# The first two output-projection groups summed in HBM, by accumulating DMAs

## The chip, the cores and the metric

The kernel runs on one core of a Trainium2 chip. The metric is device time in microseconds (us) of one execution, lower is better.

## What is computed

One layer of a decoder trunk on x of 1024 tokens by 1024 channels, all in float32. Cut to what matters here:

```python
h = rms_norm(x, norm_mix_g); z = h @ w_in
y_pool = pooling_mixer(z[:, :512])                 # 4 groups of 128 channels
y_attn = rms_norm(diff_attention(q, k, v)) * 0.8   # 4 heads of 128 channels
y = concat(y_pool, y_attn)                         # 1024 x 1024
x = x + y @ w_out                                  # the output projection
h = rms_norm(x, norm_ffn_g)
gu = h @ ffn_w_in; g = conv3(gu[:, :2816]); u = gu[:, 2816:]
x = x + (silu(g) * u) @ ffn_w_out
return rms_norm(x, norm_final_g)
```

## The kernel before

Every matrix product is done as three float32r products of a high and a low part ("split": a ScalarE cast gives the high part, a subtraction on GpSimd or VectorE the low part). The work goes through five stages.

1. **Start.** Eight row tiles of x (128 tokens each, 512 KB) are loaded by SP (line 169, four buffers), normalised (lines 114 to 130) and transposed by TensorE into hTh and hTl (lines 132 to 140). The order of the first loads is written out in LOADS (line 35): x0, g, x1, x2, the weights q0 and k0, small parameters, x3, v0. Rows x4 to x7 follow when a buffer is free. The first three projections (first_units, lines 237 to 257) run on row tiles as they arrive, in two halves of 512 tokens.
2. **Projections, attention and pooling**, in the order of PLAN (line 37).
3. **Output projection** (out_rows, line 530). The eight 128-channel pieces of y are summed in three groups, OUT_GROUPS = ((3, 2), (1, 0, 4), (5, 6, 7)) (line 33), because the last head is ready last; groups 0 and 1 fill TensorE beside the attention of head 3. For each row tile t of a group, line 533 loads the running sum (x for group 0, the scratch tensor x1_d after that), TensorE computes two halves of 512 columns into PSUM, VectorE adds each half to the loaded tile (line 541), and for groups 0 and 1 ScalarE's queue stores the tile to x1_d (line 543). The row tiles rotate through four buffers (tag "x", line 523). The weights and y pieces of a group are split in out_weights (line 465).
4. **Second norm and the blocks for the up projection.** Group 2 runs row tile by row tile with norm2 (line 561): square sums, a store of the tile to x1_d (line 568), and the scaling in place (line 577). Then transposes give the blocks b11, b21, b22 and, from differences of two row tiles (pair_blocks, line 587), t1 to t4. The feed-forward up projection uses a seven-product scheme over these blocks (ffn_up, line 656); the weights of each of the 22 column tiles are loaded by SP as ru and rg (line 621, two buffers of tag "rw"), combined and split in up_weights (line 616). up_weights runs one column tile ahead of ffn_up (lines 689 to 694).
5. **Down projection** (ffn_down, line 740) and the final norm (finish, line 713).

The order of the instructions on each engine is not written by hand: a list scheduler simulates the program and puts the ready instruction of highest priority next, priority being program order apart from stretches marked high. A ready instruction that stands later in the program can so be issued before an earlier one that still waits; afterwards each engine's order is fixed. SP, ScalarE and GpSimd each issue their DMAs in their own order; a waiting instruction holds up what is behind it on its queue.

Of the kernel before, what the change touches and what calls it, by code (L numbers as in the profile page):

```python
# [9 lines left out]
F32 = mybir.dt.float32  # L10
F32R = mybir.dt.float32r
AF = mybir.ActivationFunctionType
ALU = mybir.AluOpType
PSUM = bass.MemoryType.PSUM

P = 128
S = 1024
D = 1024
KC = D // P
NT = S // P  # L20
# [9 lines left out]
DOWN = [3] * 6 + [4]  # L30
PRODUCTS = "1675243"
QK = 10
OUT_GROUPS = ((3, 2), (1, 0, 4), (5, 6, 7))
FIRST = ("q0", "k0", "v0")
LOADS = "x0 g x1 x2 q0 k0 s x3 v0"
# [7 lines left out]
def trunk_kernel(ctx, tc, x, norm_mix_g, w_in, pool_w, rows, line, rel_bias, w_out, norm_ffn_g,  # L43
                 ffn_w_in, ffn_w_out, norm_final_g, onehot, out):
    nc = tc.nc
    x, out, w_in, w_out = x[0], out[0], w_in[0], w_out[0]
# [4 lines left out]
    x1_d = nc.dram_tensor("x1_rows", (S, D), F32).ap()  # L51

    const = ctx.enter_context(tc.tile_pool(name="const", bufs=1))
# [8 lines left out]
    def slot(dt, name):  # L62
        return slots.tile([P, S], dt, tag="y", name=name)
# [78 lines left out]
    def mm3(ps, wh, wl, hh, hl, first, last):  # L142
        nc.tensor.matmul(ps, wh, hh, start=first, stop=False)  # L143
        nc.tensor.matmul(ps, wh, hl, start=False, stop=False)  # L144
        nc.tensor.matmul(ps, wl, hh, start=False, stop=last)  # L145


    nc.scalar.preload_act_table_set("natural_log_exp_and_others")
    ident = const.tile([P, P], F32, name="ident")
    make_identity(nc, ident)  # L150
    flip = const.tile([P, P], F32, name="flip")
# [35 lines left out]

    prm = const.tile([P, 96], F32, name="prm")
    gsub = const.tile([P, 1], F32, name="gsub")
    nlam = const.tile([P, 1], F32, name="nlam")  # L190

    def small_params():
# [20 lines left out]

    g_bc = att.tile([P, D], F32, tag="qk", bufs=QK, name="g_mix")
    hTh = [big.tile([P, 4, S], F32R, tag="h", name=f"hTh{q}") for q in range(2)]
# [16 lines left out]
    def first_bank(n, half):  # L232
        ps = (sc_ps if n == "v0" else mm_ps)(f"z_{n}_{half}")
        first_ps[n, half] = ps
        return ps

    def first_units(qt):
        half = qt // 2
        if half:
            if qt == 3:  # L240
                for n in FIRST:
                    proj_half(first_bank(n, 1), *first_w[n], 1)
                    with tc.high_priority():
                        first_evac[n](1, first_ps[n, 1])
            return
        for n in FIRST:
            if qt % 2 == 0:
                first_bank(n, half)
            ps = first_ps[n, half][:, (qt % 2) * 256:(qt % 2) * 256 + 256]
            wh, wl = first_w[n]  # L250
            cs = slice(qt * 256, qt * 256 + 256)
            for k in range(KC):
                mm3(ps, wh[:, k, :], wl[:, k, :], hTh[k // 4][:, k % 4, cs], hTl[k // 4][:, k % 4, cs],
                    k == 0, k == KC - 1)
            if qt % 2:
                with tc.high_priority():
                    first_evac[n](half, first_ps[n, half])
# [4 lines left out]
    def proj_half(ps, wh, wl, half):  # L262
        cs = slice(half * 512, half * 512 + 512)
        for k in range(KC):
            mm3(ps, wh[:, k, :], wl[:, k, :], hTh[k // 4][:, k % 4, cs], hTl[k // 4][:, k % 4, cs],
                k == 0, k == KC - 1)
# [9 lines left out]
    def q_sink(h):  # L276
        q = [att.tile([P, S], F32R, tag="qk", bufs=QK, name=f"q{h}_{c}") for c in range(2)]

        def evac(half, ps):
            cs = slice(half * 512, half * 512 + 512)  # L280
            for c in range(2):
                hi = q[c][64 * c:64 * c + 64, cs]
                lo = q[c][64 - 64 * c:128 - 64 * c, cs]
                src = ps[64 * c:64 * c + 64, :]
                nc.scalar.mul(hi, src, SC)
                nc.vector.scalar_tensor_tensor(lo, src, SC, hi.bitcast(F32), op0=ALU.mult, op1=ALU.subtract)
        return q, evac

    def k_sink(h):
        kh = [(slot(F32R, f"kh{h}_{c}") if h == 1 else  # L290
               att.tile([P, S], F32R, tag="qk", bufs=QK, name=f"kh{h}_{c}")) for c in range(2)]
        kl = slot(F32R, f"kl{h}") if h == 1 else att.tile([P, S], F32R, tag="qk", bufs=QK, name=f"kl{h}")

# [10 lines left out]
    def v_sink(h):  # L304
        vh = att.tile([P, S], F32R, tag="qk", bufs=QK, name=f"vh{h}")
        if h == 1:
            vl = slot(F32R, f"vl{h}")
        else:
            vl = att.tile([P, S], F32R, tag="pl" if h == 3 else "qk", bufs=3 if h == 3 else QK, name=f"vl{h}")
        vh, vl = [a.rearrange("p (t e) -> p t e", e=P) for a in (vh, vl)]  # L310
# [10 lines left out]
    for t in range(NT):  # L321
        if t == 1:
            first_w.update({n: split_w(first_raw[n], n) for n in FIRST})
            q0, first_evac["q0"] = q_sink(0)
            k0, first_evac["k0"] = k_sink(0)
            v0, first_evac["v0"] = v_sink(0)
            small_params()
        if t not in xs:
            xs[t] = load_x(t)
        xt = xs[t]  # L330
        sq = att.tile([P, S], F32, tag="pl", bufs=3, name=f"sq_{t}")
        r = row_rstd(xt, sq, f"m{t}")
        scale_rows(xt, xt, r, g_bc, t in SHARE)
        with tc.high_priority():
            to_channels(xt, hTh, hTl, t, "m")
        if t % 2 == 1:
            first_units(t // 2)

    yT = [None] * 8

# [124 lines left out]
    def out_weights(gi):  # L465
        wo = []
        for n, k in enumerate(OUT_GROUPS[gi]):
            raw = ws.tile([P, D], F32, tag="raw", bufs=1, name=f"wo_{k}") if gi == 0 else e_tile(F32, f"wo_{k}")
# [56 lines left out]
    def e_tile(dt, name):  # L525
        return wide.tile([P, S], dt, tag="e", bufs=2, name=name)

    x1 = [None] * NT

    def out_rows(gi, wo, t):  # L530
        ts = slice(t * P, (t + 1) * P)
        xt = x1[t] = x_tile(F32, f"x1_{gi}_{t}")
        nc.sync.dma_start(xt, (x1_d if gi else x)[ts, :])
        for half in range(2):
            cs = slice(half * 512, half * 512 + 512)
            ps = mm_ps(f"o_{gi}_{t}_{half}")
            for n, (yh, yl, wh, wl) in enumerate(wo):
                nc.tensor.matmul(ps, yh[:, ts], wh[:, cs], start=n == 0, stop=False)  # L538
                nc.tensor.matmul(ps, yh[:, ts], wl[:, cs], start=False, stop=False)  # L539
                nc.tensor.matmul(ps, yl[:, ts], wh[:, cs], start=False, stop=n == len(wo) - 1)  # L540
            nc.vector.tensor_tensor(xt[:, cs], xt[:, cs], ps, op=ALU.add)  # L541
        if gi < 2:
            nc.scalar.dma_start(x1_d[ts, :], xt)

    for s in OUT_PLAN.split():
        if s[0] == "w":
# [69 lines left out]
    def up_weights(ct):  # L616
        raw = []
        for n, c in (("u", NCT + ct), ("g", ct)):
            r = mid.tile([P, KC * P], F32, tag="rw", bufs=2, name=f"r{n}{ct}")
            src = ffn_w_in[:, c * P:(c + 1) * P].rearrange("(k p) c -> p k c", p=P)  # L620
            nc.sync.dma_start(r.rearrange("p (k c) -> p k c", c=P), src)
            raw.append(r)
        u, g = raw
        a11, a12, a21, a22 = u[:, 0:512], u[:, 512:1024], g[:, 0:512], g[:, 512:1024]
        sa = mid.tile([P, S], F32, tag="st", bufs=2, name=f"sa{ct}")
        sb = mid.tile([P, S], F32, tag="st", bufs=2, name=f"sb{ct}")
        s1, s2, s3, s4 = sa[:, 0:512], sa[:, 512:1024], sb[:, 0:512], sb[:, 512:1024]
        nc.gpsimd.tensor_tensor(s1, a21, a22, op=ALU.add)  # L628
        nc.vector.tensor_tensor(s2, s1, a11, op=ALU.subtract)  # L629
        nc.vector.tensor_tensor(s4, a12, s2, op=ALU.subtract)  # L630
        nc.gpsimd.tensor_tensor(s3, a11, a21, op=ALU.subtract)
        uh, ul = u_tile(F32R, f"uh{ct}"), u_tile(F32R, f"ul{ct}")
        split(uh, ul, u)
        gt = x_tile(F32R, f"gt{ct}")
        split(gt[:, 0:512], gt[:, 512:1024], a22, nc.vector)
        sh = []
        for n, t in (("a", sa), ("b", sb)):
            h, l = (u_tile if n == "a" else x_tile)(F32R, f"s{n}h{ct}"), u_tile(F32R, f"s{n}l{ct}")
            split(h, l, t, nc.vector)
            sh.append((blocks(h), blocks(l)))  # L640
        (ah, al), (bh_, bl_), (uh, ul), gb = sh[0], sh[1], (blocks(uh), blocks(ul)), blocks(gt)
        return {"1": (uh[:, 0], ul[:, 0], "b11"), "2": (uh[:, 1], ul[:, 1], "b21"), "3": (bh_[:, 1], bl_[:, 1], "b22"),
                "4": (gb[:, 0], gb[:, 1], "t4"), "5": (ah[:, 0], al[:, 0], "t1"), "6": (ah[:, 1], al[:, 1], "t2"),
                "7": (bh_[:, 0], bl_[:, 0], "t3")}
# [112 lines left out]
    ct = 0  # L757
# [68 lines left out]
```

## Time and profile before

| what | value |
|---|---|
| time, median of 3 runs | 1114.7 us (1113.57 to 1114.74) |
| the profiled execution, device time | 1115.49 us |
| its span in the profile | 1113.7 us |
| TensorE busy (PE) | 96% of the span |
| VectorE busy (DVE) | 66% |
| ScalarE busy (ACT) | 43% |
| GpSimd busy (POOL) | 31% |
| HBM read, written | 82.57 MB, 28.32 MB |

Outside the profiled span lie 1115.49 - 1113.7 = 1.8 us of the profiled execution. Its device time is 0.8 us above the median of the three runs. Busy shares are means over five stages with different limits, so the profile is read stage by stage.

### The profile page before, as it was taken

How to read it: one execution, taken by the hardware profiler on the slowest of the kernel's cores; microseconds unless marked ns; L12 is line 12 of the kernel's file. 1: busy time of each engine (PE TensorE's matmuls, PEld its weight loads, DVE VectorE, ACT ScalarE, POOL GpSimd, SP SyncE). 2: the span in 40 equal slices, each digit the busy share in tenths (PEclk: the TensorE clock that was granted, in tenths of full speed). 3: DMA queues.
4: the chain of work that ended last, by engine and by line, in shares of the span. 5: the costliest groups of instructions: out<-in, count | busy, mean ns of one | idle time of the engine just before them, and what ended most of it. 6: DMA issues, size and time to landing. Idle time of an engine off the chain costs nothing.

```text
span 1113.7 us, 13597 instructions
## 1 busy us (share of the span) xinstructions
PE 1066.6 (96%) x5011; PEld 884.0 (79%) x5011; DVE 732.3 (66%) x1213; ACT 475.9 (43%) x775; POOL 341.7 (31%) x240
## 2 busy tenths in 40 slices
PE   5999999999899997999999999999999999999997
PEld 4988888887677675878888888888888788888885
DVE  7556787877797689577657656755665655544545
ACT  5557476655752355244333443443344222111133
POOL 3232242433730247133312232221314322221211
PEclk9999999999899998999999999999999999999999
DMA  8010110110386742123122212222247632212112
GB/s 242 28 50 27 43 46 19 43 39 26 133 278 216 242 171 76 57 95 95 57 94 95 93 59 96 90 81 76 82 127 267 223 114 99 89 60 95 39 50 102
DMA packets 85990, 111.76 MB, mean 100 GB/s; under 512 B 3618, under 2 KB 66303, under 8 KB 85924
## 3 DMA queue, kind: packets, MB, share of 16 engines
q1 hardware_dynamic: 79300, 86.78, 24.4%
q10 hardware_dynamic: 6624, 24.12, 5.5%
q8 instruction: 39, 0.64, 0.2%
q14 instruction: 27, 0.22, 0.1%
HBM read 82.57 MB, written 28.32 MB: 100 GB/s over the span
## 4 chain that ended last, share of the span: by engine, by line
PE 81%; DVE 8%; issue 4%; DMA 3%; ACT 1%; POOL 1%; SPq 1%; DVEq 0%; ACTq 0%; POOLq 0%
PE p L650 36%; PE fo L747 7%; PE fo L749 7%; PE fo L748 7%; PE tpa L402 1%; PE z_q L144 1%; PE z_q L145 1%; PE z_q L143 1%; PE o L538 1%; PE o L539 1%; PE o L540 1%; PE z_p L143 1%; PE z_p L144 1%; PE z_p L145 1%; PE z_v L143 1%
## 5 line engine op out<-in xcount | busy, mean ns | idle before, releaser
L747 PE MATMUL fo<-w,a 128*128 128x512 f32 x352 | 137.3, 390 | 2.8 <-DVE xr L750 2.8
L750 DVE TENSOR_TENSOR xr<-xr,fo 128x512 f32<-128x512 f32 x112 | 75.9, 684 | 97.0 <-PE fo L749 96.3
L748 PE MATMUL fo<-w,a 128*128 128x512 f32 x352 | 137.0, 389 | 0.0
L749 PE MATMUL fo<-w,a 128*128 128x512 f32 x352 | 137.0, 389 | 0.0
L80 POOL TENSOR_TENSOR w<-rw,w 128x1024 fp32r<-128x1024 f32 x22 | 61.3, 2796 | 156.4 <-ACT w L79 151.1
L628 POOL TENSOR_TENSOR sa<-rg 128x512 f32<-128x512 f32 x22 | 32.9, 1495 | 209.8 <-DMA rg<-in_ffn_w_in_dram 201.3
L80 POOL TENSOR_TENSOR ul<-ru,uh 128x1024 fp32r<-128x1024 f32 x22 | 58.1, 2642 | 71.8 <-PE p L650 37.6
L747 PEld LDWEIGHTS fo<-w,a 128*128 128x128 f32 x352 | 66.1, 188 | 17.6 <-DVE xr L750 4.0
L749 PEld LDWEIGHTS fo<-w,a 128*128 128x128 f32 x352 | 66.1, 188 | 13.9
L748 PEld LDWEIGHTS fo<-w,a 128*128 128x128 f32 x352 | 66.1, 188 | 13.6
L79 ACT CAST a<-ra 128x1024 fp32r<-128x1024 f32 x22 | 23.1, 1051 | 118.8 <-DVE xr L750 64.1
L362 ACT ACTIVATE p<-p,nm 128x128 f32<-128x128 f32 (+7 forms) x64 | 49.6, 776 | 40.9 <-DVE nm L361 40.5
L650 PE MATMUL p<-t4h,gt 128*128 128x512 f32 x176 | 58.9, 396 | 1.7 <-DVE g L675 1.7
L629 DVE TENSOR_TENSOR sa<-sa,ru 128x512 f32<-128x512 f32 x22 | 39.9, 1814 | 21.1 <-POOL sa L628 21.1
L538 PE MATMUL o<-woh,yh 128*128 128x512 f32 x128 | 51.9, 409 | 1.6 <-DVE x L541 1.4
L349 POOL CAST qz<-q 64x128 fp32r<-64x128 f32 x64 | 24.5, 384 | 92.3 <-PE s L353 85.4
L79 ACT CAST uh<-ru 128x1024 fp32r<-128x1024 f32 x22 | 23.2, 1054 | 68.0 <-PE p L650 67.4
L539 PE MATMUL o<-wol,yh 128*128 128x512 f32 x128 | 50.6, 397 | 1.4 <-POOL wol L80 1.4
L677 DVE TENSOR_TENSOR g<-eb,p 128x512 f32<-128x512 f32 x22 | 15.1, 687 | 55.5 <-PE p L650 55.5
L80 DVE TENSOR_TENSOR a<-ra,a 128x1024 fp32r<-128x1024 f32 x22 | 43.0, 1956 | 12.1 <-ACT a L79 11.6
L540 PE MATMUL o<-woh,yl 128*128 128x512 f32 x128 | 50.0, 393 | 0.9 <-DVE yl L80 0.9
L79 ACT CAST gt<-rg 128x512 fp32r<-128x512 f32 x22 | 13.7, 623 | 82.1 <-PE p L650 75.1
(264 smaller groups left out, 3111.0 us busy)
## 6 DMA issues: line engine op xcount, KB each, us to landing
x_rows<-x ACTq DMA_DIRECT2D x24, 512.0 KB, 3.6
ru<-in_ffn_w_in_dram SPq DMA_DIRECT2D x22, 512.0 KB, 4.0
rg<-in_ffn_w_in_dram SPq DMA_DIRECT2D x22, 512.0 KB, 3.9
act_rows<-cv ACTq DMA_DIRECT2D x22, 512.0 KB, 2.6
rw<-in_ffn_w_out_dram SPq DMA_DIRECT2D x22, 512.0 KB, 4.4
ra<-act_rows SPq DMA_DIRECT2D x22, 512.0 KB, 3.4
x<-in_x_dram SPq DMA_DIRECT2D x16, 512.0 KB, 5.6
x<-x_rows SPq DMA_DIRECT2D x16, 512.0 KB, 3.7
```

The costliest lines, as they stand in the source:

```text
L79: nc.scalar.copy(hi, src)
L80: (lo_eng or nc.gpsimd).tensor_tensor(lo, src, hi.bitcast(F32), op=ALU.subtract)
L362: nc.scalar.activation(s[:, 0:w], s[:, 0:w], AF.Exp, bias=negm[:, c:c + 1], accum_out=sums[:, c:c + 1])
L538: nc.tensor.matmul(ps, yh[:, ts], wh[:, cs], start=n == 0, stop=False)
L539: nc.tensor.matmul(ps, yh[:, ts], wl[:, cs], start=False, stop=False)
L540: nc.tensor.matmul(ps, yl[:, ts], wh[:, cs], start=False, stop=n == len(wo) - 1)
L629: nc.vector.tensor_tensor(s2, s1, a11, op=ALU.subtract)
L650: nc.tensor.matmul(ps, w[:, k, :], h[:, k, :], start=start and k == 0 and n == 0, stop=k == 3 and n == 2, skip_group_check=not start)
L747: nc.tensor.matmul(ps, ah[:, ts], wh[:, cs], start=n == 0, stop=False)
L748: nc.tensor.matmul(ps, ah[:, ts], wl[:, cs], start=False, stop=False)
L749: nc.tensor.matmul(ps, al[:, ts], wh[:, cs], start=False, stop=n == len(ops) - 1)
L750: nc.vector.tensor_tensor(xr[t][:, cs], xr[t][:, cs], ps, op=ALU.add)
```

## The change

- Two pads of 32 bytes per partition move the identity tile and the constants behind gsub in SBUF.
- After the start loop, SP copies x to x1_d inside HBM, in eight DMAs of 512 KB.
- In groups 0 and 1 nothing is loaded and nothing is added on VectorE: ScalarE copies each half out of PSUM, and GpSimd issues a DMA that adds the tile to x1_d in HBM. Group 2 still loads x1_d and adds on VectorE.
- For the first two column tiles of the up projection, VectorE writes one column into each raw weight tile ahead of its load, taken from row tile 1 (column tile 0) or row tile 7 (column tile 1). The load then has to wait for that write, and so for that row tile. The load overwrites the column.

```diff
+PADS = (8, 8)
...
     nc.scalar.preload_act_table_set("natural_log_exp_and_others")
+    const.tile([P, PADS[0]], F32, name="pad0")
     ident = const.tile([P, P], F32, name="ident")
...
     gsub = const.tile([P, 1], F32, name="gsub")
+    const.tile([P, PADS[1]], F32, name="pad1")
     nlam = const.tile([P, 1], F32, name="nlam")
...
         if t % 2 == 1:
             first_units(t // 2)
+
+    for t in range(NT):
+        nc.sync.dma_start(x1_d[t * P:(t + 1) * P, :], x[t * P:(t + 1) * P, :])
...
     def out_rows(gi, wo, t):
         ts = slice(t * P, (t + 1) * P)
         xt = x1[t] = x_tile(F32, f"x1_{gi}_{t}")
-        nc.sync.dma_start(xt, (x1_d if gi else x)[ts, :])
+        if gi == 2:
+            nc.sync.dma_start(xt, x1_d[ts, :])
...
-            nc.vector.tensor_tensor(xt[:, cs], xt[:, cs], ps, op=ALU.add)
+            if gi == 2:
+                nc.vector.tensor_tensor(xt[:, cs], xt[:, cs], ps, op=ALU.add)
+            else:
+                nc.scalar.copy(xt[:, cs], ps)
         if gi < 2:
-            nc.scalar.dma_start(x1_d[ts, :], xt)
+            nc.gpsimd.dma_start(x1_d[ts, :], xt, accum_op=ALU.add)
...
             r = mid.tile([P, KC * P], F32, tag="rw", bufs=2, name=f"r{n}{ct}")
+            if ct < 2:
+                nc.vector.tensor_copy(r[:, 0:1], x1[(1, NT - 1)[ct]][:, D - 1:D])
             src = ffn_w_in[:, c * P:(c + 1) * P].rearrange("(k p) c -> p k c", p=P)
```

## Rows read from the trace of the kernel before

**Rows 1.** The page, busy us of TensorE, share of the span, instructions.

```profile
PE 1066.6 (96%) x5011; PEld 884.0 (79%) x5011; DVE 732.3 (66%) x1213; ACT 475.9 (43%) x775; POOL 341.7 (31%) x240
```

**Rows 2.** Stretches: length, busy PE, PEld, DVE, ACT, POOL, PE clock, DMA share, GB/s.

```profile
302.00:350.00 48.00, 45.19 (x224) 36.36 (x224) 45.43 (x95) 23.84 (x39) 13.08 (x9) 1.00 0.71 250
350.00:377.00 27.00, 27.00 (x139) 22.95 (x138) 12.92 (x21) 6.81 (x11) 1.93 (x2) 1.00 0.55 199
377.00:392.00 15.00, 11.61 (x45) 7.53 (x43) 10.83 (x14) 4.71 (x11) 5.41 (x2) 1.00 0.79 246
...
420.00:446.00 26.00, 19.55 (x87) 14.85 (x86) 25.43 (x33) 14.06 (x29) 20.34 (x11) 0.82 0.22 75
```

**Rows 3.** Whom TensorE waited for, 376 to 446: us, times, longest.

```profile
PE tp_b L584 <- DVE x L577: 3.9, 3, 2.7
...
PE o L539 <- POOL wol L80: 1.4, 2, 1.0
```

**Rows 4.** Single lines' instructions: ns min/median/max, first and last start, forms.

```profile
L541 DVE TENSOR_TENSOR x<-x,o x48: 671/680/691, 301.6 to 422.9; 128x512 f32<-128x512 f32 x48
...
L543 ACTq DMA_DIRECT2D x_rows<-x x16: 326/326/341, 302.9 to 377.5; - x16
...
L669 ACT COPY ea<-p x22: 578/588/593, 436.1 to 844.9; 128x512 f32<-128x512 f32 x22
```

**Rows 5.** The issues on SP in order of time: start, us, line, what.

```profile
11.21 0.50 SPq L169 DMA_DIRECT2D x<-in_x_dram  x1
...
377.32 0.42 SPq L621 DMA_DIRECT2D ru<-in_ffn_w_in_dram  x1
```

**Rows 6.** The DMA view of 0 to 20 us, total.

```profile
DMA packets 5409, 5.71 MB, mean 285 GB/s; under 512 B 239, under 2 KB 4555, under 8 KB 5409
```

**Rows 7.** VectorE in order of time, near 24 us: start, us, line, what.

```profile
24.47 1.28 DVE L130 SCALAR_TENSOR_TENSOR x<-x,rr_m,g_mix 128x1024 f32<-128x1024 f32 x1
```

**Rows 8.** TensorE in order of time, 30 to 43 us.

```profile
30.48 0.60 PE L139 MATMUL tp_m<-ident,x 128*128 128x128 f32 x4
...
43.00 0.60 PE L139 MATMUL tp_m<-ident,x 128*128 128x128 f32 x4
```

**Rows 9.** GpSimd in order of time, near 376 us.

```profile
376.36 6.05 POOL L80 TENSOR_TENSOR wol<-wo,woh 128x1024 fp32r<-128x1024 f32 x2 [9.19 <-DMA x_rows<-x]
```

**Rows 10.** Line 568, the eight stores of norm2, issue to landing.

```profile
DMA to landing us min/median/max: 2.6/2.8/5.7
```

**Rows 11.** VectorE in order of time, 396 to 443 us.

```profile
396.93 1.29 DVE L577 SCALAR_TENSOR_TENSOR x<-x,rr_f,g_ffn 128x1024 f32<-128x1024 f32 x1
...
420.81 1.28 DVE L577 SCALAR_TENSOR_TENSOR x<-x,rr_f,g_ffn 128x1024 f32<-128x1024 f32 x1
...
434.54 1.70 DVE L577 SCALAR_TENSOR_TENSOR x<-x,rr_f,g_ffn 128x1024 f32<-128x1024 f32 x1
...
439.61 2.84 DVE L596 TENSOR_TENSOR ta<-x,ta 128x512 f32<-128x512 f32 x1
```

**Rows 12.** GpSimd in order of time, near 439 us.

```profile
438.73 3.16 POOL L80 TENSOR_TENSOR ul<-ru,uh 128x1024 fp32r<-128x1024 f32 x1 [0.73 <-ACT uh L79]
```

**Rows 13.** TensorE in order of time, 443 to 448 us (in brackets: idle before).

```profile
443.19 0.75 PE L584 MATMUL tp_t<-ident,tb 128*128 128x128 f32 x4 [2.49 <-DVE t2l L84]
...
445.04 0.63 PE L650 MATMUL p<-b11h,uh 128*128 128x512 f32 x1
...
447.32 0.39 PE L650 MATMUL p<-b11h,uh 128*128 128x512 f32 x1
```

**Rows 14.** VectorE in order of time, 290 to 296 us.

```profile
290.42 3.27 DVE L390 SCALAR_TENSOR_TENSOR p<-p,rc,p 128x128 f32<-128x128 f32 x1
...
295.06 0.48 DVE L390 SCALAR_TENSOR_TENSOR p<-p,rc,p 128x256 f32<-128x256 f32 x1 [0.57 <-ACT p L389]
```

**Rows 15.** GpSimd in order of time, near 289 us.

```profile
288.86 4.68 POOL L80 TENSOR_TENSOR yl<-yT,yh 128x1024 fp32r<-128x1024 f32 x2
```

**Rows 16.** ScalarE in order of time, near 421 us.

```profile
421.27 1.06 ACT L79 CAST uh<-ru 128x1024 fp32r<-128x1024 f32 x1 [0.62 <-PE o L539]
```

## The prediction

> **What bounds the kernel now.** I read the page first: TensorE is busy for 1066.6 of 1113.7 us [rows 1]. So no stage can win more than TensorE's idle time in it, and the time that a lower clock costs. I then cut the span into stretches around the lines that the change touches [rows 2]. In 302 to 350, where groups 0 and 1 run beside the last head, TensorE lacks 2.81 us of 48, while VectorE is busy for 45.43: VectorE is the second limit there. From 350 to 377 TensorE has no gap at all. From 377 to 392, where group 2 begins, 3.39 of 15 us are idle. From 420 to 446, the change to the feed-forward stage, 6.45 of 26 are idle, the granted clock is 0.82, and VectorE is busy for 25.43: that is the only stretch where a large piece lies open. What ends these gaps is VectorE's scaling and GpSimd's splits of output weights [rows 3], and VectorE's t2l [rows 13].
>
> **The change, part by part.** Removed: 16 loads on SP, 32 of the 48 adds of line 541 (32 x 0.68 = 21.8 us of VectorE) and 16 stores on ScalarE's queue (0.326 us each) [rows 4]. Added: 32 ScalarE copies, 0.588 us each by the same copy of PSUM in line 669 [rows 4], 18.8 us over the 75 us of both groups, where ScalarE is busy for half or less [rows 2]; 16 accumulating DMAs on GpSimd's queue; 8 copies inside HBM on SP; 4 VectorE copies of one column, each under the 0.68 us of a 512-column add.
>
> *A, the copies at the start.* They need nothing, so the scheduler can issue them once the twelve first loads are out; I expect them ahead of x4, which SP issues at 11.21 [rows 5]. Eight times 512 KB are 4.19 MB; at the 285 GB/s of the first 20 us [rows 6] that is 14.7 us during which x4 waits behind them. x4 was scaled by 24.47 + 1.28 = 25.75 [rows 7] and transposed at 30.48 [rows 8], a slack of 4.7, which leaves 10.0. The last tile is transposed from 43.00 on; between lie 12.5 us of TensorE, of which six groups of transposes at 0.60 [rows 8] take 3.6; 8.9 are projections of rows 0 to 3, which can go first. If the scheduler orders them so, 1.1 us stay, and x5 to x7 come behind with 1.28 us of scaling each against 1.20 of transposes: 3 x 0.08 = 0.2. Ends: 0 (the copies behind x7, where the queues are free) and +10.0 (TensorE's order as before). I take **+1.3**, since a scheduler that simulates the loads sees x4 late.
>
> *B, groups 0 and 1.* A gain can't be more than the 2.81 us of idle time in 302 to 350 [rows 2]. VectorE loses most of the 21.8 us there, but the attention chain also passes ScalarE, which now waits for TensorE where VectorE waited before, with exponentials and casts queued behind the copies; and GpSimd, where casts of q and splits of weights stand behind accumulations that wait for ScalarE. I take half, **-1.4**; ends -2.8 and +1.4. The four row buffers come free later if an accumulation takes longer than a store, but the load ahead of the sum is gone, and in 350 to 377 three further row tiles stand between two uses, of 18 matmuls each at 27.00 / 139 = 0.19 us [rows 2], 10 us in all: nothing, up to a landing of that length.
>
> *C, the end of group 1.* GpSimd splits the last two weight tiles in 6.05 us from 376.36 on [rows 9], and TensorE waits 1.4 us for them [rows 3]. The last two accumulations stand in the same queue at that time. The trace has no DMA issue on GpSimd. The nearest rows are the issue on ScalarE's queue, 0.326 [rows 4], and a full GpSimd instruction, about 3.0 (half of 6.05): ends 0 (if both are put behind the splits) and 2 x 3.0 = 6.0. I take 2 x 0.33 = **+0.7**, by the row that is also a DMA issue.
>
> *D, the first weight load.* ru and rg of column tile 0 are issued at 377.32 [rows 5], in the middle of a stretch with a DMA share of 0.79 [rows 2], and are not cast until 421.27 [rows 16]. Held until row tile 1 is scaled, at 396.93 + 1.29 = 398.2 [rows 11], they leave the rings to group 2's first rows: the slowest store of norm2, 5.7 us, falls to the median of 2.8 [rows 10], and the scaling of row 0 that waits for it comes up to 2.9 us sooner. TensorE was idle there for only part of that (its three waits for scaling are 3.9 in all, the longest, 2.7, for a later row [rows 3]): **-0.8**, ends -1.2 and 0. Behind the two loads on SP's queue stand the loads of group 2's last rows, which wait for free buffers; I take nothing; if they come at the same time, 1 MB at 285 GB/s is +3.7.
>
> *E, the second weight load.* It waits for row tile 7, scaled by 434.54 + 1.70 = 436.2 [rows 11]. Now its low part, 3.16 us on GpSimd, starts at 438.73 [rows 12], beside row tile 7's own VectorE work: t2 takes 2.84 us [rows 11] where an add of that size takes 0.68 [rows 4]. With the split moved past it, 2.84 - 0.68 = 2.16 of the 2.49 us that TensorE waits for t2l [rows 13] go. After that wait TensorE ran at the lower of its two levels (1.2 instead of 2.4 GHz): its matmuls are 0.63 us long at 445.04 and 0.39 at 447.32 [rows 13]. From the end of the wait at 443.19 to some point between these two rows, say 446.8, that costs half, 1.8 us; I take 1.0 of it. Together **-3.2**, ends -4.3 and +2.0 (what is late next are column tile 1's own products; the cover is column tile 0's 7 x 12 = 84 matmuls, 16 us at 0.19; if the order puts tile 1 early, the gap comes back). The pads and the column copies: nothing shown in either direction, **0**, ends -1 and +1 (transposes read the identity, but no row shows a time that goes with an address).
>
> The sum is 1.3 - 1.4 + 0.7 - 0.8 - 3.2 = **-3.4**. From the profiled execution's 1115.5 that gives 1112.1. It stood 0.8 above the median of its runs, so the forecast for a median is **1111.3**.
>
> The Trainium skill, DMA: Bandwidth & Descriptors, section "SWDGE vs HWDGE vs iDMA", says that accumulation is possible only from GpSimd, whose descriptors are written by software, and its section "Specifications" gives about 1 us to the first byte against 0.6 from SP or ScalarE. By 1 us per issue as an estimate, C would be +2.0 and the time 1112.6; no run here shows it yet.
>
> **The rivals.**
> 1. *The copies cost their full price (slower).* Place: SP's queue between v0 and x4. If TensorE's order stays and x4 lands 14.7 us later, A is 10.0 and the sum +5.3: **1120.0**. It decides from A above about 7. For it: the rings run without a gap until x4 has landed [rows 6]. Against it: 8.9 us of other work. Chance 0.16.
> 2. *GpSimd becomes the gate (slower).* If an accumulation holds GpSimd as long as a split, C is 6.0 and B +1.4: sum +4.7, **1119.4**. For it: VectorE and GpSimd slow each other here, a VectorE instruction over 128 columns took 3.27 us, against 0.48 over 256 later [rows 14], while GpSimd ran two splits in 4.68 [rows 15]. Against: GpSimd is busy for only 13 of 48 us in 302 to 350 [rows 2]. Chance 0.11. The Trainium skill, SBUF — State Buffer, section "Who interferes with whom", says that a DMA issued by GpSimd can be starved while VectorE holds the port pair that the two share; the rows just named agree as to compute instructions, and none shows it for a DMA.
> 3. *Nothing moves.* TensorE is full in 350 to 377 and VectorE's free time is only waiting time; the gap at 443 is made by the three-step chain of differences whatever runs beside it. B and E are 0, the sum +1.2: **1115.9**. Chance 0.16.
> 4. *The first wait isn't the one meant.* Row tile 1 and row tile 5 share a buffer of four. If the column is taken when tile 5 is there, scaled by 422.1 [rows 11], the load lands some 4 us later, at 426, and uh moves from 421.27 [rows 16] by 5: with 4.0 of it on the path the sum is +0.6, **1115.3**. Chance 0.07.
>
> **How the numbers follow.** The forecast has 0.50, with a range of its own of 1106.4 (the lower ends of all five, -8.3) to 1113.5. About 0.2%, 2.2 us, is what a measurement of this kernel can tell from no change: faster is below 1112.5, slower above 1116.9. Faster: 0.46 of the forecast and 0.01 of rival 3. Same: the forecast's 0.04, rivals 3 and 4 for 0.21. Slower: rivals 1 and 2 and a tail of rival 4, 0.28. The range reaches from 1105.4 (with -1 for the pads) to 1120.5, past rival 1.
>
> **What would show it.** In the changed profile: the HBM copies ahead of x4 on SP, and transposes of x4 after 30.5 with projections before them (A); VectorE well under 45 of the 48 us beside the last head (B); short DMA issues on GpSimd and a wait for wol of about 2 us (C); ru and rg after 398, and stores of norm2 near 2.8 (D); t2 in 0.7 to 1.3 us and no wait of 2.5 for t2l (E). I am wrong if the first stage ends more than 5 us later, if casts of q or splits stand behind accumulations for microseconds while TensorE is idle, or if the gap at 443 only moves.

## The result, and the profile after

The changed kernel takes **1129.2 us** (median of 4 runs, 1127.2 to 1130.2) against 1114.1 for the kernel before: 1.0133 times as long, 95% interval 1.0115 to 1.0150, some 15 us slower. The forecast was 1111.3 with a range from 1105.4 to 1120.5. The profiled execution took 1128.36 us; its span is 1126.1, 12.4 longer than before.

The page of the changed kernel, busy us, share and instructions of each engine:

```profile
PE 1075.6 (96%) x5011; PEld 886.6 (79%) x5011; DVE 705.6 (63%) x1185; ACT 493.4 (44%) x807; POOL 347.4 (31%) x256
```

Beside [rows 1], VectorE lost 26.7 us of work, as meant. But TensorE's busy time *rose* by 9.0 us with the same 5011 matmuls. Matmuls that take longer are a sign that idle time alone can't explain, so I cut the span again. First stretches of the kernel before, in the columns of [rows 2], chosen where the changed kernel differs:

```profile
18.00:45.00 27.00, 25.90 (x197) 25.08 (x198) 20.95 (x47) 18.50 (x41) 8.39 (x8) 1.00 0.27 84
45.00:60.00 15.00, 15.00 (x68) 12.29 (x67) 4.27 (x10) 4.49 (x9) 2.68 (x2) 1.00 0.16 46
620.00:720.00 100.00, 100.00 (x443) 82.79 (x442) 66.88 (x66) 41.35 (x49) 28.90 (x17) 1.00 0.27 85
900.00:1060.00 160.00, 160.00 (x707) 132.50 (x706) 80.99 (x94) 29.58 (x31) 41.25 (x15) 1.00 0.25 86
```

The same stretches after:

```profile
18.00:45.00 27.00, 22.88 (x172) 21.85 (x172) 16.37 (x41) 15.21 (x36) 5.73 (x7) 1.00 0.65 225
45.00:60.00 15.00, 12.23 (x49) 9.83 (x50) 8.36 (x14) 4.32 (x9) 2.89 (x3) 0.67 0.05 14
620.00:720.00 100.00, 100.00 (x438) 82.07 (x437) 63.99 (x62) 39.83 (x48) 29.35 (x16) 1.00 0.24 77
900.00:1060.00 160.00, 160.00 (x707) 132.50 (x706) 81.05 (x93) 31.36 (x32) 41.26 (x15) 1.00 0.25 86
```

Two losses show. **The start**: TensorE idles 4.1 and 2.8 us, and from 45 to 60 the granted clock is 0.67, a mean of the two levels, so that about two thirds of that stretch ran at 1.2 instead of 2.4 GHz, behind the gaps (before: 1.1 us idle, none, and clock 1.00). The first score matmul of attention stands at 55.3 instead of 45.7, 9.6 us late, and nothing behind it makes that up: the last output-projection matmul comes 9.7 us late (432.2, before 422.4). **The up projection**: TensorE is full in 620 to 720 in both kernels at the full clock, yet issues 438 matmuls instead of 443. In the down projection (900 to 1060) the rate is the same.

What the forecast was about came in part. Whom TensorE waited for after, 376 to 490:

```profile
PE tp_b L594 <- DVE x L587: 4.4, 1, 4.4
PE o L545 <- DVE x L549: 2.2, 3, 1.3
PE p L662 <- DVE rt_f L110: 0.6, 1, 0.6
```

Beside [rows 3, 13], the waits for wol (1.4) and for t2l (2.5) are gone. From the last output-projection matmul to the last one of the up projection (875.6, before 865.7) both kernels take 443 us, so that what the slower matmuls cost there the change of stages gave back. A gain in groups 0 and 1 doesn't show. Their stretch, which begins some 10 us later, in the same columns:

```profile
312.00:360.00 48.00, 44.73 (x229) 36.87 (x229) 32.36 (x78) 35.45 (x64) 21.66 (x20) 1.00 0.75 144
```

VectorE is busy for 32.36 us instead of 45.43 [rows 2], but TensorE lacks 3.27 of the 48, not less than the 2.81 before. Behind the up projection another 2.5 us are lost: where the down projection begins, TensorE's longest wait is 2.6 us instead of 1.0 and the clock from 867 to 900 is 0.95. Why was not traced. So the work of the change was done and part of its gains came, and something else cost 15 us and more.

### The profile page after: what moved, and what is told of

It reads as the page before. It is cut to its first block, busy times and chain, and to the rows that moved or that the text cites. A ratio compares the mean times of both kernels' runs of the same rounds, so it can differ in the third digit from the quotient of the medians.

```text
span 1126.1 us, 13587 instructions
## 1 busy us (share of the span) xinstructions
PE 1075.6 (96%) x5011; PEld 886.6 (79%) x5011; DVE 705.6 (63%) x1185; ACT 493.4 (44%) x807; POOL 347.4 (31%) x256
## 4 chain that ended last, share of the span: by engine, by line
PE 80%; DVE 6%; DMA 5%; issue 4%; ACT 2%; POOL 2%; SPq 1%; DVEq 0%; ACTq 0%; POOLq 0%
PE p L662 36%; PE fo L759 7%; PE fo L760 7%; PE fo L761 7%; PE tpa L408 1%; PE o L545 1%; PE s L359 1%; PE s L358 1%; PE z_p L144 1%; PE z_q L144 1%; PE z_p L146 1%; PE z_p L145 1%; PE o L546 1%; PE z_q L145 1%; PE z_q L146 1%
## 5 line engine op out<-in xcount | busy, mean ns | idle before, releaser
L689 DVE TENSOR_TENSOR g<-eb,p 128x512 f32<-128x512 f32 x22 | 15.1, 688 | 56.0 <-PE p L662 56.0
## 6 DMA issues: line engine op xcount, KB each, us to landing
x_rows<-in_x_dram SPq DMA_DIRECT2D x8, 512.0 KB, 10.8
```

## The experiments

Every kernel ran beside the kernel before on the same chip; ratios are to that kernel, with a 95% interval. Medians of before were 1112.4 to 1113.9 us. Runs on different chips are compared by their ratios.

### The copies at the start

The kernel before with the copies alone:

```diff
+    for t in range(NT):
+        nc.sync.dma_start(x1_d[t * P:(t + 1) * P, :], x[t * P:(t + 1) * P, :])
```

> The kernel before with the eight copies inside HBM alone (group 0 overwrites them later). Theory: five of the copies stand ahead of x4 on SP, the last transposes of the start end 8 to 10 us later, and as nothing behind it makes that up the time is 1123 to 1125. Rival 'the late start is absorbed and the loss arises at the output groups': within 2 us of 1114. Spacing of matmuls in the up projection as before (443 per 100 us) by the theory, 438 if the copies make it.

Measured: 1124.7 us, ratio 1.0105 (1.0087 to 1.0123); 443 matmuls in 620 to 720. The copies alone cost 11.5 us (1124.66 - 1113.16). In that run too the first score matmul comes late, at 55.0, and the clock from 45 to 60 is 0.66. How it comes about, the changed kernel's trace shows. Issues on SP in order of time: start, us, line, what:

```profile
11.17 4.14 SPq L343 DMA_DIRECT2D x_rows<-in_x_dram  x5
15.44 0.49 SPq L171 DMA_DIRECT2D x<-in_x_dram  x1
15.98 3.66 SPq L343 DMA_DIRECT2D x_rows<-in_x_dram  x3
20.63 0.38 SPq L92 DMA_DIRECT2D raw_q<-in_w_in_dram  x1
22.18 2.78 SPq L200 DMA_DIRECT2D bias_row<-r_sb  x1
25.05 4.80 SPq L171 DMA_DIRECT2D x<-in_x_dram  x3
```

Five copies go ahead of x4 and three between x4 and x5. x5 was issued at 17.00 before:

```profile
17.00 0.33 SPq L169 DMA_DIRECT2D x<-in_x_dram  x1
```

Now it is at 25.05. The weight and the small store stood ahead of it before, too; new are the eight copies, whose issues alone hold SP for 4.14 + 3.66 = 7.8 us. The DMA view of 11 to 30, KB each and median us to landing:

```profile
x_rows<-in_x_dram SPq DMA_DIRECT2D x8, 512.0 KB, 10.8
x<-in_x_dram SPq DMA_DIRECT2D x4, 512.0 KB, 10.5
```

Before, in the same stretch:

```profile
x<-in_x_dram SPq DMA_DIRECT2D x4, 512.0 KB, 5.4
```

VectorE's scalings of x4 to x7 in the changed kernel, in order of time (the first of a shared pair is line 128):

```profile
28.89 1.29 DVE L131 SCALAR_TENSOR_TENSOR x<-x,rr_m,g_mix 128x1024 f32<-128x1024 f32 x1
...
42.02 0.75 DVE L128 TENSOR_SCALAR x<-x,rr_m 128x1024 f32<-128x1024 f32 x1
...
44.20 2.13 DVE L131 SCALAR_TENSOR_TENSOR x<-x,rr_m,g_mix 128x1024 f32<-128x1024 f32 x1
...
46.25 0.74 DVE L128 TENSOR_SCALAR x<-x,rr_m 128x1024 f32<-128x1024 f32 x1
```

Against [rows 7], x4 is only 4.4 us late. The kernel before scales x5 here:

```profile
26.89 0.74 DVE L127 TENSOR_SCALAR x<-x,rr_m 128x1024 f32<-128x1024 f32 x1
```

Now x5 is 15.1 us late (8.05 of it by its later issue), and x6 and x7 are 12.1 and 10.6 late (before at 32.11 and 35.67). TensorE uses up its projections of rows 0 to 3 and then waits, 6.05 us in these four gaps (in brackets: idle before, and for whom):

```profile
43.19 0.66 PE L320 MATMUL tpv<-ident,vt 128*128 128x128 f32 x4 [2.13 <-ACT vt L317]
45.31 1.97 PE L140 MATMUL tp_m<-ident,x 128*128 128x128 f32 x8 [1.46 <-POOL x L129]
49.10 1.97 PE L140 MATMUL tp_m<-ident,x 128*128 128x128 f32 x8 [1.82 <-DVE hTl L85]
51.71 1.94 PE L140 MATMUL tp_m<-ident,x 128*128 128x128 f32 x8 [0.64 <-DVE hTl L85]
```

The transposes themselves show the price of the gaps: four took 0.60 [rows 8], eight take 1.97, in the stretch whose clock is 0.67. The other direction, the changed kernel with its copies held back to 200 us later:

```diff
-    for t in range(NT):
-        nc.sync.dma_start(x1_d[t * P:(t + 1) * P, :], x[t * P:(t + 1) * P, :])
...
+    def late_copies(src):
+        for t in range(NT):
+            rows_t = slice(t * P, (t + 1) * P)
+            nc.sync.dma_start(x1_d[rows_t, 0:1], src[:, 0:1])
+            nc.sync.dma_start(x1_d[rows_t, :], x[rows_t, :])
...
+        if s == "p3":
+            late_copies(yT[3])
```

> The changed kernel with the eight HBM copies held back until y piece 3 is there (each behind a one-column transfer from that tile to the same rows, which the copy overwrites). Theory: the start is as before (last transposes near 45), 8 to 10 us less than the changed kernel, 1119 to 1121; what is left above 1114 is the slower matmuls. Rival 'GpSimd's accumulations are the cost': no more than 3 us less than the changed kernel. If the late copies delay group 0's loads of weights, 1 to 3 us of it comes back.

Measured: 1113.7 us, ratio 1.0006 (0.9996 to 1.0016). Holding the copies back wins more than expected, 1.0133 - 1.0006 = 1.27%, 14 us, and with it the changed kernel is as fast as the one before. TensorE is full in 45 to 60 again, at clock 1.00. So the accumulations and the waits together have no large net cost.

The copies alone, on ScalarE's queue in place of SP's (one word of the diff above):

> The kernel before with the eight HBM copies alone, issued from ScalarE's queue instead of SP's. On SP they cost 11.5 us (1124.7). Theory 'order on SP': x4 to x7 keep their places on SP; if only that counts, 1113 to 1115. Rival 'the copies' bytes': 4.19 MB still share the 16 DMA engines with x4 to x7, so those land 5 to 10 us late all the same, 1119 to 1124. ScalarE also loses eight issues of about 0.33 us between its square sums.

Measured: 1128.1 us, ratio 1.0151 (1.0121 to 1.0181), no faster than on SP. But the question was not answered: on that queue the copies went out first of all, and the loads of x did not keep their places on SP either. The first copies on ScalarE's queue, then x3 on SP's, which the changed kernel issues at 10.30:

```profile
0.77 1.96 ACTq L340 DMA_DIRECT2D x_rows<-in_x_dram  x3
```

```profile
25.37 0.35 SPq L169 DMA_DIRECT2D x<-in_x_dram  x1
```

So this run tells only that the copies cost as much at that earlier place. How much of the 11.5 us is bytes and how much place on the queue stays open.

### The pads

The kernel before with both pads, and the changed kernel without them:

```diff
+    const.tile([P, 8], F32, name="pad0")
     ident = const.tile([P, P], F32, name="ident")
...
     gsub = const.tile([P, 1], F32, name="gsub")
+    const.tile([P, 8], F32, name="pad1")
```

> The kernel before with the two pads alone. Theory (the start copies cost 9 to 10 us, and the pads, by moving every tile behind them in SBUF, make the matmuls of the projections and of the up projection about 1% slower, 4 to 5 us): 1118 to 1119 us, with 438 instead of 443 matmuls per 100 us in 620 to 720. Rival 'the slower matmuls come from the accumulating DMAs or from the new order': 1114 us, 443 per 100 us. Rival 'GpSimd's accumulations are the cost': also 1114.

Measured: 1117.4 us, ratio 1.0038 (1.0023 to 1.0052), 438 matmuls.

> The changed kernel without the two pads. Theory: 4 to 5 us less than the changed kernel, 1124 to 1125, with 443 matmuls per 100 us in 620 to 720. Rival 'the pads do nothing': 1129, 438 per 100 us.

Measured: 1122.1 us, ratio 1.0084 (1.0065 to 1.0102), 443 matmuls. So 64 bytes per partition that nobody reads cost 4.2 us alone and 1.0133 / 1.0084, 0.49% or 5.4 us, in the changed kernel. Then the pads one at a time, the second and the first:

> The kernel before with the second pad alone (behind gsub; the identity stays where it was). If every tile allocated behind a pad moves by 32 bytes and any such move makes the matmuls slower: 1117, 438 matmuls per 100 us in 620 to 720. If it is the first pad (the identity and all behind it) or only the sum of both that matters: 1113, 443 per 100 us.

> The kernel before with the first pad alone: the identity and everything allocated behind it move by 32 bytes. If what counts is how far the tiles behind the constants moved (32 bytes, as with the second pad alone): 1125 to 1126, 430 matmuls per 100 us in 620 to 720. Rival 'each pad has its own effect, and the first one, by moving the identity, gains 8 us (both pads 1117, second alone 1126)': about 1105. Rival 'only the second pad matters': 1112 to 1113.

Measured: 1125.7 (ratio 1.0118, 1.0099 to 1.0137) and 1125.0 (1.0107, 1.0090 to 1.0124). One pad costs about *three times* as much as both, and it doesn't matter whether the identity moves. With the second pad alone the up projection begins at 429.2 (before 429.0) and its last matmul stands at 876.1 (865.7), so the loss lies in that stage. The lines of the windows view of that run:

```profile
620.00:720.00 100.00, 100.00 (x430) 80.48 (x429) 62.21 (x62) 38.88 (x47) 26.56 (x15) 1.00 0.26 84
900.00:1060.00 160.00, 160.00 (x708) 132.57 (x707) 81.12 (x94) 31.36 (x32) 41.25 (x15) 1.00 0.25 86
```

What counts is the sum of the pads, which three more sizes behind gsub pursue (one pad of 64, 128 and 96 bytes):

> The kernel before with one pad of 64 bytes behind gsub, the identity unmoved. If the total shift counts: as both pads of 32 bytes, 1117, 438 matmuls per 100 us. If the identity's place counts: 1126 or another value.

> The kernel before with one pad of 128 bytes behind gsub. 32 bytes gave 1125.6, 64 bytes 1117.0. If the rate depends on the address within 128 bytes, it is as with no pad: 1113, 443 matmuls per 100 us in 620 to 720. If any shift from the place before costs: 1117 or more.

> The same with 96 bytes. If the rate depends on the address within 64 bytes: as 32, 1125 to 1126, 430 per 100 us. If within 128 bytes: a value of its own, above 1113.

Measured: 1117.0 (1.0043, 1.0023 to 1.0063), 1124.7 (1.0101, 1.0088 to 1.0114) and 1126.1 (1.0121, 1.0105 to 1.0136). One pad of 64 bytes is as two of 32; neither 64 nor 128 bytes is a period. What is left is where the two operands of a matmul lie. SBUF is allocated from both sides. In the up projection the blocks b and t come from the left, which the pads move (pool h2), and the weights from the right (pool wide); in the down projection both operands come from h2. So a pad at the right end, alone and with one of 32 bytes behind gsub:

```diff
+    edge = ctx.enter_context(tc.tile_pool(name="edge", bufs=1, side="right"))
+    edge.tile([P, 8], F32, name="pad_r")
```

> The kernel before with a pad of 32 bytes at the other end of SBUF: the tiles allocated from the right side (in the up projection, those of weights) move by 32 bytes towards the others, and the tiles on the left side (there, the blocks b and t) stay. If the rate goes with the distance between a matmul's two operands: as with 32 bytes on the left, 1125, 430 matmuls per 100 us in 620 to 720. If it goes with the address of the left tiles alone: 1113, 443. In both cases the down projection, whose operands both lie on the left, stays at 707 matmuls in 900 to 1060.

> The kernel before with a pad of 32 bytes on each side, so that the distance shrinks by 64 bytes. If the distance counts: as with 64 bytes on the left, 1117, 438 per 100 us. If the address of the left tiles alone counts: as with 32 bytes on the left, 1125, 430.

Measured: 1125.5 (1.0109, 1.0093 to 1.0125) and 1118.1 (1.0034, 1.0022 to 1.0046). The windows of the two, the right pad alone first:

```profile
620.00:720.00 100.00, 100.00 (x430) 80.33 (x429) 62.98 (x62) 39.36 (x46) 27.04 (x15) 1.00 0.26 82
```

```profile
620.00:720.00 100.00, 100.00 (x438) 82.05 (x438) 65.79 (x65) 40.01 (x48) 27.37 (x16) 1.00 0.27 85
```

The address of the left tiles alone is out: moving the other side does the same, and 32 on each side is as 64 on one. All of it fits the distance, though only one case moved both sides.

| operands nearer by | tried as | us | matmuls, 620 to 720 |
|---|---|---|---|
| 0 | the kernel before | 1112.4 to 1113.9 | 443 |
| 32 bytes | pad left (two places), right | 1125.7, 1125.0, 1125.5 | 430, 431, 430 |
| 64 bytes | 32 + 32 left, 64 left, 32 on each side | 1117.4, 1117.0, 1118.1 | 438, 439, 438 |
| 96 bytes | left | 1126.1 | 430 |
| 128 bytes | left | 1124.7 | 432 |

### The groups and the waits

The changed kernel with late copies and without pads:

> The changed kernel with the HBM copies held back, and without the pads. Theory (start copies, pads and the rest add up, and the pads are worth the 4.2 us that they cost alone): 1109 to 1110 us, 443 matmuls per 100 us in 620 to 720, 3 to 4 below the kernel before. Rival 'without the late start the pads cost nothing': 1113 to 1114.

Measured: **1108.4 us**, ratio 0.9965 (0.9952 to 0.9978), 443 matmuls, faster than both kernels; below it is the fast version. From here single parts were taken away. First both waits (the column copies):

```diff
-            if ct < 2:
-                nc.vector.tensor_copy(r[:, 0:1], x1[(1, NT - 1)[ct]][:, D - 1:D])
```

> The kernel of the run just named without the column copies, so the first two column tiles' weight loads wait for no row tile. If the waits bring the forecast's 4.0 us (D and E), it is 4 us slower than that run, 1113 to 1114, and the wait for t2l of 2.5 us is back. Rival 'the gain comes from the accumulation (VectorE free beside the last head, no loads)': the same time as that run, 1109 to 1110.

Measured: 1118.7 us, ratio 1.0057 (1.0039 to 1.0075), 10 us slower, and at another place than the t2l chain. SP's order, and TensorE at the entry of group 2:

```profile
368.26 0.50 SPq L634 DMA_DIRECT2D ru<-in_ffn_w_in_dram  x1
368.80 0.89 SPq L634 DMA_DIRECT2D rg<-in_ffn_w_in_dram  x1
369.79 4.01 SPq L543 DMA_DIRECT2D x<-x_rows  x1
```

```profile
384.66 0.80 PE L548 MATMUL o<-woh,yh 128*128 128x512 f32 x1 [6.30 <-DVE x L552]
```

With the loads of groups 0 and 1 gone from SP, the first up weights move up to just ahead of group 2's first row tile, whose load lands late; TensorE waits 6.3 us. The last three accumulations land later, too, after 10.6 us at the median, in the fast version after 7.8. The first wait, which puts these weights at 389 in the fast version, prevents that. Each wait alone:

> The changed kernel with late copies, no pads, and the first column tile's wait alone. Both waits gave 1108.4, none 1118.7, and without the first wait the weight loads stood ahead of group 2's first row. Theory: the first wait brings nearly all of it once the row tiles come back by accumulation: 1108 to 1111. Rival 'the second wait (t2l) is worth the forecast's 3.2': 1111.5 to 1113.

> The same with the second column tile's wait alone. Theory: the first weight load stands ahead of group 2's first row again, TensorE waits about 6 us there: 1115 to 1119. Rival 'the second wait carries the gain': 1108 to 1110.

Measured: 1114.9 (1.0009, 0.9997 to 1.0021) and 1114.2 (1.0008, 0.9997 to 1.0018). Against none (1.0057) and both (0.9965), the first wait is worth 0.48% or 0.43%, the second 0.49% or 0.44%, about 5 us each; the first expectation gave too much to the first. The windows show one gap for each. The first wait alone:

```profile
377.00:392.00 15.00, 14.45 (x67) 11.43 (x66) 10.13 (x26) 6.26 (x19) 2.01 (x2) 1.00 0.69 199
420.00:446.00 26.00, 18.22 (x69) 14.23 (x70) 24.97 (x32) 12.43 (x20) 11.41 (x7) 0.76 0.31 95
```

The second wait alone:

```profile
377.00:392.00 15.00, 8.38 (x28) 6.72 (x29) 4.95 (x12) 3.30 (x10) 0.00 (x0) 0.77 0.65 212
420.00:446.00 26.00, 22.10 (x102) 16.98 (x101) 23.80 (x40) 14.77 (x30) 14.88 (x9) 0.87 0.26 82
```

Without the first, 6.6 of 15 us are idle at the entry of group 2; without the second, 7.8 of 26 at the change to the up projection, and in either the clock falls; with both waits, in the fast version, it is 0.6 and 4.9:

```profile
377.00:392.00 15.00, 14.44 (x72) 11.78 (x71) 11.16 (x30) 7.44 (x23) 3.58 (x3) 1.00 0.70 215
420.00:446.00 26.00, 21.10 (x90) 16.32 (x91) 22.46 (x30) 10.35 (x16) 8.42 (x6) 0.87 0.25 67
```

What the second wait takes away is a wait of TensorE of 2.5 us for t3h. Without it VectorE's scaling of row tile 7 takes 3.16 us beside GpSimd's split for column tile 1; with it, alone, 1.28.

The kernel before with both waits and nothing else:

> The kernel before with the column copies alone. If the waits bring D and E: 1109 to 1110. Rival 'the waits only move the gap (row-tile scaling is late next)': 1112 to 1114. Rival 'a late first load holds up group 2's loads behind it on SP': 1115 or more.

Measured: 1112.3 us, ratio 0.9997 (0.9982 to 1.0013): no change. There the wait for t2l goes too, but TensorE waits at other places near it, 2.8 for row statistics and 1.5, 1.6 and 1.4 for the blocks and uh: the second rival, the gap that moves. Last, accumulation in group 1 alone, group 0 as before, no copies:

```diff
-        nc.sync.dma_start(xt, (x1_d if gi else x)[ts, :])
+        if gi != 1:
+            nc.sync.dma_start(xt, (x1_d if gi else x)[ts, :])
```

> The changed kernel without pads and without HBM copies: group 0 as in the kernel before (x loaded, added on VectorE, stored), only group 1 copied by ScalarE and accumulated by GpSimd's DMAs, both row-tile waits kept. With all groups accumulated and late copies it was 1108.4. Theory (the gain lies at the change of groups and in the waits, and needs no copies): 1107 to 1110. Rival 'the gain comes from VectorE being free beside the last head, which is group 0 and the first rows of group 1': 1110 to 1113.

Measured: 1115.7 us, ratio 1.0021 (1.0011 to 1.0030), slower than before, so group 1 alone doesn't bring the gain. Beside the last head the two differ; group 1 alone, then the fast version:

```profile
302.00:345.00 43.00, 41.00 (x208) 33.39 (x208) 40.35 (x87) 23.69 (x41) 14.10 (x10) 1.00 0.62 204
```

```profile
302.00:345.00 43.00, 42.63 (x224) 35.98 (x223) 31.25 (x74) 33.45 (x59) 21.53 (x19) 1.00 0.83 161
```

With group 0 on VectorE that engine is busy for 40.35 of 43 us and TensorE lacks 2.0; without it, 31.25 and 0.37. That is 1.6 of some 6 us between the two runs. The rest, and what group 1 alone loses against the waits alone (2.4 thousandths), were not traced.

## Why the prediction was wrong

**A, the copies at the start: wrong, and most of the miss.** I took +1.3; alone they cost 11.5, in the changed kernel 13 to 14 (1.0084 / 0.9965 and the late copies above; the intervals of these overlap). The step that failed is "1.1 us stay, and x5 to x7 come behind with 1.28 us of scaling each against 1.20 of transposes: 3 x 0.08 = 0.2". It put the whole delay on x4 and let the others follow for nothing. The trace shows the reverse: x4 is 4.4 late, inside its slack of 4.7, and x5 is 15.1 late, because all eight copies are issued ahead of it and its load lands in 10.5 us instead of 5.4. The cover was there, projections did go first, but 8.9 us cannot hide three tiles that come 10.6 to 15.1 late. The upper end of +10.0 was too low as well: it counted idle time, and the granted clock of 0.67 afterwards was in no term. Rival 1 was right that the copies delay the start by 10 us or so; but it put the delay on x4 and kept TensorE's order, and neither was so. At 0.16 it got too little.

**The pads: wrong.** The step was "The pads and the column copies: nothing shown in either direction, **0**, ends -1 and +1". They cost 4.2 alone and about 5 in place. No row of before could have given the size. But I thought only of the transposes, which read the identity, where every tile behind the pad moves; and bounds of 1 us for something that touches 409 us of full TensorE time ([rows 4], line 669 from 436.1 to 844.9) assume a change below 0.25%. The rates explain the sum: 5 of 438 matmuls on 409 us are 4.7 us, 13 of 430 are 12.4 (measured with one pad: 11.8 and 13.3).

**B, right in kind, too small, and not in the changed kernel itself.** I took -1.4 with a ceiling of 2.81. In the changed kernel TensorE's idle time there did not shrink (3.27). In the fast version TensorE is busy for 47.63 of 48 us, 2.44 more than in [rows 2], nearly the ceiling:

```profile
302.00:350.00 48.00, 47.63 (x256) 40.51 (x255) 31.49 (x75) 35.48 (x63) 22.40 (x20) 1.00 0.82 155
```

**C, price wrong, path right.** A GpSimd issue takes 0.865 us, not 0.33. From the line's own view of the changed kernel (ns min/median/max; then landing in us):

```profile
L553 POOL DMA_DIRECT2D x_rows<-x x16: 856/865/1013, 314.2 to 388.7; - x16
...
DMA to landing us min/median/max: 5.2/6.1/8.1
```

It cost nothing: of the last two issues one stands between the last two splits of wol and one behind them (385.54 and 388.71; the splits start at 383.19 and 386.37), and TensorE waits for wol nowhere. Rival 2 fell with the late copies: GpSimd waited 27.6 us for ScalarE's copies, no engine waited for an accumulation, and TensorE waited for GpSimd only 0.5 us, for a cast of q. The landing of 6.1 us, against 2.8 of the stores of norm2 [rows 10], stayed under the 10 us that I had allowed. The Trainium skill, DMA: Bandwidth & Descriptors, section "Specifications", gives about 1 us to the first byte, which I had set beside my price. That is nearer to 0.865 than the row that I chose, but it is another quantity than the time that an issue holds its engine, so the agreement is chance; no run here shows a first byte.

**D and E, right in sum only with the rest of the change.** I took -0.8 and -3.2. On the kernel before, both together are 0 (from -2.0 to +1.4 us). Beside accumulation each is worth about 5. For D the step that failed is its reason: I saw stores of norm2 that land sooner. They landed after 4.2 us in the changed kernel and 3.7 in the fast version, later than the 2.8 before [rows 10], and the real effect is that the weights no longer stand ahead of group 2's first row tile, which the removal of 16 loads from SP had let them do. I had counted those loads as a gain and not asked what would move up into their place. For E the step held in kind: with the split moved past it, row tile 7's own VectorE work is short again. Beside accumulation, however, the wait that this removes is the 2.5 us for t3h, not the one for t2l. Rival 4 fell: in the fast version the column copy of ru stands at 388.85, right behind the second scaling (387.05, 1.28 us long), so the first wait is for row tile 1. Rival 3 held on the kernel before, where E gave nothing, and not beside accumulation.

B to E were -4.7 in the forecast and are -3.9 (-5.3 to -2.4) in the fast version. That the sum is nearly right is luck: accumulation without the waits cost 6.3 us (1.0057, late copies included) where B and C were -0.7, and the waits beside it brought 10 where D and E were -4.0. The copies' 13 to 14 us, the pads' 5 and these -3.9 make up the 15 us of the result. So the time was lost on the two terms that I thought harmless, the helpers of the change.

## What to carry to other kernels

Price the set-up of a change like the change itself: transfers that need nothing are issued as early as the queue allows, ahead of what the start waits for; give them something to wait for. When instructions leave a queue, ask which later ones will take their place. After any change that moves the allocation, compare the number of matmuls in a stretch where TensorE is full; if it fell at the full clock, as here, look at the addresses, too, and not at the schedule alone.

## What the runs showed of the hardware

- The rate of 128 x 512 float32r matmuls with operands on the two sides of SBUF changed with the distance between them: 443, 430, 438, 430 and 432 per 100 us at 0, 32, 64, 96 and 128 bytes less. The down projection, with both operands on one side, kept 707 to 708 per 160 us in all of them. Why, and which distance is best, was not tried.
- Copies of 512 KB inside HBM landed after 10.8 us, and loads of x issued among them after 10.5 instead of 5.4.
- An accumulating DMA of 512 KB held GpSimd for 0.865 us and landed after 6.1 (medians of 16).
